# Norm factors of the retention moved from GpSimd to ScalarE and VectorE, and its decay factors made ahead, in a two-layer encoder trunk

## The chip, the cores and the metric

The kernel runs on one core of a Trainium2 chip. The engines are TensorE (PE, matmuls), ScalarE (ACT), VectorE (DVE), GpSimd (POOL) and SyncE (SP, which only issues DMAs). The metric is the device time of one execution, in microseconds, and the change is judged by the median of several executions.

## The reference

Two requests of 512 tokens by 1024 features go through two layers, each x + Mixer(RMSNorm(x)), and a last RMSNorm. The first mixer is differential attention, the second a retention that looks in both directions; both have 8 heads of width 256 in their values, and a gate. The change touches the second only:

```python
def rms_norm(x, g, eps):
    xf = x.astype(jnp.float32)
    y = xf * lax.rsqrt(jnp.mean(xf * xf, axis=-1, keepdims=True) + eps)
    return (y * g.astype(jnp.float32)).astype(x.dtype)
...
def bidir_retention(h, w_in, decay_fwd, decay_bwd, subln_g, w_out):
    B, S, _ = h.shape
    proj = h @ w_in
    q, k, v, gate = jnp.split(proj, [RET_QK_WIDTH, 2 * RET_QK_WIDTH, 2 * RET_QK_WIDTH + D_INNER], axis=-1)
    q = retention_rotate(q.reshape(B, S, N_HEADS, RET_QK_DIM))
    k = retention_rotate(k.reshape(B, S, N_HEADS, RET_QK_DIM)) * (RET_QK_DIM ** -0.5)
    v = v.reshape(B, S, N_HEADS, RET_V_DIM)
    log_g_f = -jnp.exp(decay_fwd.astype(jnp.float32))
    log_g_b = -jnp.exp(decay_bwd.astype(jnp.float32))
    o_f = retention_direction(q, k, v, log_g_f, True)
    o_b = jnp.flip(retention_direction(jnp.flip(q, 1), jnp.flip(k, 1), jnp.flip(v, 1), log_g_b, False), 1)
    o = rms_norm(o_f + o_b, subln_g, SUBLN_EPS)
    o = o.reshape(B, S, D_INNER) * jax.nn.silu(gate)
    return o @ w_out
```

`retention_direction` multiplies the scores of a head with powers of its decay: exp(distance x log_g), with one log_g for keys behind the query and one for keys ahead. The head's output, 256 wide, is normed (divided by the root of its mean square plus 1e-5), gated and projected back. The scale of 256 stands outside the root in the kernel: its factor is (sum of squares + 256 x 1e-5) to the power of -1/2.

## The kernel before, in words

All matmuls are done in three passes: an operand is split into a hi part (a cast on ACT, L437) and a lo part (a subtraction on DVE, L440), and hi x hi, hi x lo and lo x hi are added in a PSUM bank. All large products are done with seven products of half-size blocks instead of eight (P1 to P7, in the order of `SEQ`), whose operands are sums of blocks.

There are four stages: the input and layer 1's projections and attention, until about 1060 us; layer 2's projections; the retention with its output projection, from about 1515 us; and at its end the final norm. The first stage is not touched.

**Projections.** A `Unit` is 256 columns of the weights for both requests. `units2` makes 8 units of q and k, 8 of gates and 4 wide ones of v, and `mixed` interleaves them. `projections` is a generator with one step per product: `prep` makes the operands some steps ahead, `product` the matmuls, `evac` the sums and what follows, and the results go through the ring of slots `os` to DRAM. The last `LEFT` steps (4) are not taken before the retention but in its first rounds, one each. The last unit's bank `z` is taken from the tag "tp".

**Retention.** There are 16 blocks (a head and a request), each with 4 tiles of 128 tokens, so 64 rounds. In a round `score2` makes a tile of scores for the next block (L1228, three matmuls of 512), which DVE multiplies by the decay factors `F` (L1232) and which are split (hi and lo). `av2` multiplies a tile of the present block with v (L1246, twelve matmuls of 256). `norm_stats` has ACT square the result with a sum along the row (L790), and POOL add the constant (L794) and take the power -1/2 (L795). `norm_apply` multiplies the tile by this factor on ACT (L804, into one of two buffers `on`). One round later `turn_o` transposes it on PE (L810) and `gate2` multiplies by the gate on DVE (L1297) and makes the operands of the output projection. `fill` puts one or two output products (`out2`, L1353, six matmuls of 512) into each round.

**Decay factors.** `decay(h)`, called in the retention when a head comes up first, loads the table of distances (448 KB) into `F0` or `F1`, makes on DVE the part of the block on the diagonal (L1209, L1211, L1213) and takes three exponentials on ACT (L1214, L1216, L1218).

**Output weights.** They are split for four heads' worth at a time by `w_split`: P1, P2 and P3 load a block on SP's queue into the tile `wa` or `wb`; P5, P6 and P4 (in `wa`) and P7 (in `wb`) add a block to what stands there, with an accumulating DMA, which POOL issues (L1268, `b<-in_ret_w_out_dram`). Then the sum is split in hi and lo (a cast of 128x1024 on ACT and a subtraction on DVE). Each is made when the old one was used last, so three times in the retention, after the first time at its start. The results of the output products are added to x in DRAM by accumulating DMAs too, issued by POOL at the same line (L1268, `x<-b`) from buffers that DVE (L1378, `put`) or ACT (L1390) writes; for the last heads they are added in SBUF (`evac_last`, L1407), and the final norm follows (L1257).

**What sets the order.** All operations are recorded in a `Plan`, with a cost and what they read and write. `arrange` simulates them and writes down, for each engine, one fixed order: at each step the engine that is free takes the ready operation with the earliest due time. An accumulating DMA costs 1 us of POOL there, lands 5.5 us later, and is held 5 us after it is ready. On the chip each engine works its list in this order: if an operation must wait, all behind it on this engine wait as well.

## Time and profile before

| | us |
|---|---|
| median of the three runs | 1891.86 (1891.03 to 1892.7) |
| profiled execution | 1895.15 |
| its span, first to last instruction | 1893.4 |
| PE busy | 1823.2 (96%) |
| DVE busy | 1462.6 (77%) |
| ACT busy | 967.5 (51%) |
| POOL busy | 230.8 (12%) |
| granted TensorE clock, mean | 0.988 |

An engine that is busy throughout is the limit only in the stretch that the row is for; the views that follow therefore go by stretches of the span. A timeline row gives start, length, engine, line, operation, the tile written and the tiles read; where it has brackets at its end, they hold how long the engine had stood idle and what it waited for. A row of waits gives the engine and line that waited, the engine and line waited for, and then the total in us, the number of times and the longest. A row of groups gives line, engine, operation, tiles and count, then the busy time in us and the mean in ns of one, then the idle time ahead of them. The names `b`, `arena` and `bank` stand for several buffers each.

### The profile page before, as it was taken

How to read it: one execution, taken by the hardware profiler on the slowest of the kernel's cores; microseconds unless marked ns; L12 is line 12 of the kernel's file. 1: busy time of each engine (PE TensorE's matmuls, PEld its weight loads, DVE VectorE, ACT ScalarE, POOL GpSimd, SP SyncE). 2: the span in 40 equal slices, each digit the busy share in tenths (PEclk: the TensorE clock that was granted, in tenths of full speed). 3: DMA queues.
4: the chain of work that ended last, by engine and by line, in shares of the span. 5: the costliest groups of instructions: out<-in, count | busy, mean ns of one | idle time of the engine just before them, and what ended most of it. 6: DMA issues, size and time to landing. Idle time of an engine off the chain costs nothing.

```text
span 1893.4 us, 27928 instructions
## 1 busy us (share of the span) xinstructions
PE 1823.2 (96%) x10241; PEld 1574.5 (83%) x10241; DVE 1462.6 (77%) x2451; ACT 967.5 (51%) x1973; POOL 230.8 (12%) x436
## 2 busy tenths in 40 slices
PE   6999999999999999999999999999999989897977
PEld 5888988988989888888888888989898978786866
DVE  6979688688688688888888887685868677666667
ACT  6744444343343465555556863444444466465543
POOL 2000000000000021111112100000000024443332
PEclk9999999999999999999999999999999999998989
DMA  4345545545445674444452434544455588888884
GB/s 157 119 126 178 167 134 177 157 121 180 156 136 188 250 269 165 178 165 170 178 189 91 138 101 144 167 150 162 145 167 152 194 291 221 217 221 208 237 190 133
DMA packets 161025, 326.18 MB, mean 172 GB/s; under 512 B 13028, under 2 KB 73080, under 8 KB 160888
## 3 DMA queue, kind: packets, MB, share of 16 engines
q1 hardware_dynamic: 149440, 303.36, 48.0%
q0 software_dynamic: 11264, 20.98, 6.9%
q8 instruction: 80, 1.31, 0.3%
q14 instruction: 57, 0.47, 0.1%
q10 hardware_dynamic: 184, 0.08, 0.0%
HBM read 202.72 MB, written 121.63 MB: 171 GB/s over the span
## 4 chain that ended last, share of the span: by engine, by line
PE 83%; DVE 6%; issue 3%; DMA 3%; ACT 3%; POOL 2%; SPq 0%; POOLq 0%; DVEq 0%; ACTq 0%
PE bank L628 36%; PE bank L635 16%; PE bank L879 8%; PE bank L1353 5%; PE bank L1114 5%; PE bank L1062 4%; PE bank L1246 3%; PE bank L1228 2%; PE bank L1098 1%; PE bank L810 1%; DMA b<-in_dist_dram 1%; DVE arena L440 1%; DVE b L440 1%; DMA b<-in_ret_w_out_dram 1%; DVE ws L440 1%
## 5 line engine op out<-in xcount | busy, mean ns | idle before, releaser
L628 PE MATMUL bank<-arena,ws 128*128 128x512 f32 x2160 | 516.1, 393 | 4.9 <-DVE e L495 3.0
L628 PEld LDWEIGHTS bank<-arena,ws 128*128 128x128 f32 x2160 | 405.3, 188 | 93.5 <-ACT ws L437 3.0
L628 PE MATMUL bank<-b,ws 128*128 128x512 f32 x1200 | 293.7, 391 | 0.6 <-DVE e L665 0.6
L628 PEld LDWEIGHTS bank<-b,ws 128*128 128x128 f32 x1200 | 224.7, 188 | 49.7 <-issue 1.0
L794 POOL TENSOR_SCALAR css<-css 128x1 f32<-128x1 f32 x128 | 46.0, 359 | 1522.7 <-ACT bank L792 924.1
L440 DVE TENSOR_TENSOR ws<-st,ws 128x512 fp32r<-128x512 f32 (+1 forms) x192 | 147.9, 775 | 93.3 <-ACT ws L437 59.6
L657 ACT COPY c<-bank 128x512 f32<-128x512 f32 x168 | 98.1, 585 | 219.8 <-PE bank L628 137.3
L635 PE MATMUL bank<-ws,arena 128*128 128x256 f32 x1728 | 207.7, 279 | 0.0
L635 PEld LDWEIGHTS bank<-ws,arena 128*128 128x128 f32 x1728 | 204.6, 188 | 1.3
L879 PE MATMUL bank<-ws,arena 128*128 128x512 f32 x768 | 202.1, 400 | 0.0
L440 DVE TENSOR_TENSOR ws<-raw,ws 128x512 fp32r<-128x512 f32 (+1 forms) x156 | 127.4, 822 | 74.8 <-ACT ws L437 65.7
L437 ACT CAST ws<-st 128x512 fp32r<-128x512 f32 (+1 forms) x192 | 131.9, 693 | 101.2 <-PE bank L628 56.6
L879 PEld LDWEIGHTS bank<-ws,arena 128*128 128x128 f32 x768 | 139.5, 188 | 27.2
L437 ACT CAST ws<-raw 128x512 fp32r<-128x512 f32 (+1 forms) x156 | 114.1, 738 | 75.4 <-PE bank L628 59.3
L665 DVE TENSOR_TENSOR e<-bank,c 128x512 f32<-128x512 f32 x168 | 115.2, 686 | 31.4 <-PE bank L628 24.0
L635 PE MATMUL bank<-ws,b 128*128 128x256 f32 x960 | 118.9, 279 | 0.0
L635 PEld LDWEIGHTS bank<-ws,b 128*128 128x128 f32 x960 | 115.1, 188 | 0.7
L1078 ACT ACTIVATE b<-bank,nm 128x512 f32<-128x512 f32 x128 | 88.1, 688 | 50.5 <-DVE nm L1070 50.4
L884 DVE TENSOR_TENSOR b<-bank,b 128x512 f32<-128x512 f32 x128 | 87.7, 685 | 30.8 <-PE bank L879 30.5
L1114 PE MATMUL bank<-arena 128*128 128x256 f32 x768 | 106.6, 289 | 0.0
L1062 PE MATMUL bank<-arena 128*128 128x512 f32 x384 | 99.9, 396 | 3.4 <-ACT b L1078 3.4
L1070 DVE TENSOR_REDUCE nm<-bank 128x1 f32<-128x512 f32 x128 | 86.6, 687 | 12.6 <-PE bank L1062 12.2
(156 smaller groups left out, 2830.2 us busy)
## 6 DMA issues: line engine op xcount, KB each, us to landing
qk<-os SPq DMA_DIRECT2D x192, 256.0 KB, 3.9
arena<-qk SPq DMA_DIRECT2D x80, 512.0 KB, 5.4
raw<-in_da_w_in_dram SPq DMA_DIRECT2D x64, 512.0 KB, 4.9
v<-os SPq DMA_DIRECT2D x64, 512.0 KB, 3.8
arena<-v SPq DMA_DIRECT2D x48, 512.0 KB, 4.2
raw<-in_ret_w_in_dram SPq DMA_DIRECT2D x48, 512.0 KB, 4.4
g<-e SPq DMA_DIRECT2D x48, 256.0 KB, 4.5
x<-b POOLq DMA_DIRECT2D x48, 256.0 KB, 5.8
```

What stands on the lines that cost most here:

```text
L437: act(n, lambda: nc.scalar.copy(dst(), src()), r, w)
L440: dve(n, lambda: nc.vector.tensor_tensor(dst(), src(), hi().bitcast(F32), op=ALU.subtract), r, w)
L628: nc.tensor.matmul(ps.t, a[u][0]()[:, k, :], bt[k][:, v, :], start=(opens and k == 0 and i == 0), stop=(k == 3 and i == 2), skip_group_che ...
L635: nc.tensor.matmul(ps[:, (t % 2) * 256:(t % 2) * 256 + 256], bt[k][:, v, t * P:(t + 1) * P], a[u][0]()[:, k, :], start=(opens and t % 2 == ...
L657: act(S, lambda c=c, ps=ps: nc.scalar.copy(c.t, ps.t), [ps], [c])
L665: dve(S, lambda e=e, ps=ps, c=c: nc.vector.tensor_tensor(e.t, ps.t, c.t, op=ALU.add), [ps, c], [e])
L879: nc.tensor.matmul(ps.t, o[a][:, e, t * P:(t + 1) * P], u[b][:, e, :], start=(n == 0), stop=(n == 5))
L884: dve(S, lambda: nc.vector.tensor_tensor(half, ps.t, half, op=ALU.add), [ps, (x, i)], [(x, i)])
L1062: nc.tensor.matmul(s.t, q[:, a, t * P:(t + 1) * P], k[:, b, :], start=(n == 0), stop=(n == 2))
L1078: act(840, lambda j=j, s=s, m=m: nc.scalar.activation(p[:, j, :], s.t, AF.Exp, bias=m.t, accum_out=sm[:, j:j + 1]), [s, m], [(p, j), (sm, j)])
L1114: nc.tensor.matmul(o[:, 0:256], aT[:, a, j * P:(j + 1) * P], v[b][:, j, :], start=(n == 0), stop=(n == 11))
L1353: nc.tensor.matmul(ps.t, pick(A[i], u), (hi, lo)[v][:, i, :], start=(opens and n == 0), stop=(n == 5), skip_group_check=True)
```

## The change

1. **Norm.** In the retention, `norm_two` takes the place of `norm_stats`: ACT's Square (L788 of the kernel after), then Sqrt on ACT with the constant as its bias (L790), then on DVE a reciprocal (L791) and three operations of 128x1 for one Newton step (L792, L794, L796). POOL does no norm any more outside layer 1 and the row norms.
2. **Decay factors.** `decay_table(h)` makes the factors of each head in a slot of the `os` ring during the second projections, evenly spread, and stores them in DRAM (`f_d`). `decay(h)` in the retention only loads them.
3. **Units.** `LEFT` is 2. The last wide unit goes to the end of the units; half of its results are put into arena slots 9, 10, 11 and 14 instead of the `os` ring; the bank `z` is that of the others.
4. **Places.** `F0` takes arena slot 3 and the last `aT1` the place `os2`, the other way round than before. A constant `guard` is new.

```diff
...
-LEFT = 4
+LEFT = 2
...
-    LATE = dict(q0=["raw0"], k0=["raw1"], v0=["raw2", "raw3"], aT0=["st0", "st1", "st2", "os0"], sg0=["os1"], F0=["os2"],
-                aT1=[0, 1, 2, 3], k1=[4], q1=[5], v1=[6, 7], AB=[8, 9, 10], sg1=[12], F1=[13], wa=[20], wb=[21], S4=[22],
+    LATE = dict(q0=["raw0"], k0=["raw1"], v0=["raw2", "raw3"], aT0=["st0", "st1", "st2", "os0"], sg0=["os1"], F0=[3],
+                aT1=[0, 1, 2, "os2"], k1=[4], q1=[5], v1=[6, 7], AB=[8, 9, 10], sg1=[12], F1=[13], wa=[20], wb=[21], S4=[22],
...
+    guard = const([P, 1], "guard")
+    dve(4, lambda: nc.vector.memset(guard.t, 256 * SUB_EPS), [], [guard])
...
-            self.z = "sc"
...
-                self.banks[which] = [bank(dict(x="pj", z=self.z, y="o")[which], which) for _ in range(n_banks)]
+                self.banks[which] = [bank(dict(x="pj", z="sc", y="o")[which], which) for _ in range(n_banks)]
...
-    def v_done(dst):
+    def v_done(dst, free=None):
         def done(i, g, tiles, s, psum):
             for u, x in enumerate(tiles):
-                o = os_t()
+                o = slot(next(free), [P, 2, S]) if free and i else os_t()
...
+    def norm_two(o):
+        ss, l, r, t = col(tag="css"), col(tag="crs"), col(tag="crr"), col(tag="cnt")
+        def square():
+            nc.scalar.activation(o[:, 256:512], o[:, 0:256], AF.Square, accum_out=ss.t)
+        act(550, square, [(o, 0)], [(o, 1), ss])
+        plan.op("ACT", 0.22, lambda: nc.scalar.activation(l.t, ss.t, AF.Sqrt, bias=guard.t), [ss, guard], [l])
+        dve(8, lambda: nc.vector.reciprocal(r.t, l.t), [l], [r])
+        dve(8, lambda: nc.vector.scalar_tensor_tensor(
+            t.t, ss.t, 256 * SUB_EPS, r.t, op0=ALU.add, op1=ALU.mult), [ss, r], [t])
+        dve(8, lambda: nc.vector.scalar_tensor_tensor(
+            t.t, t.t, -0.5, r.t, op0=ALU.mult, op1=ALU.mult), [t, r], [t])
+        dve(8, lambda: nc.vector.scalar_tensor_tensor(
+            r.t, t.t, 1.5, r.t, op0=ALU.add, op1=ALU.mult), [t, r], [r])
+        return r
     def norm_stats(o, scale_col=None):
...
+    f_d = [dram([P, 896], f"f{h}") for h in range(NH)]
...
-                      v_done({(i, g): v_d[1, h + i, g] for i in range(2) for g in range(NG)}))
+                      v_done({(i, g): v_d[1, h + i, g] for i in range(2) for g in range(NG)},
+                             iter((9, 10, 11, 14)) if h == NH - 2 else None))
                  for h in range(0, NH, 2)]
-        return mixed(ropes, gates, wides, 2)
+        units = mixed(ropes, gates, wides, 2)
+        last = units.index(wides[-1])
+        units[last:] = units[last + 1:] + units[last:last + 1]
+        return units
...
+    def decay_table(h):
+        t = os_t(F32, "F")
+        Fd = t.t.rearrange("p a s -> p (a s)")
+        dma(lambda: Fd[:, 0:896], lambda: dist_in, [], [t], 448)
+        mid = work("og", [P, P], 2, name="mid")
+        mid2 = work("og", [P, P], 2, name="mid")
+        dve(P, lambda: nc.vector.tensor_scalar(
+            mid.t, Fd[:, 384:512], 0.0, lr[:, 0, h:h + 1], op0=ALU.max, op1=ALU.mult), [t, lr], [mid])
+        dve(P, lambda: nc.vector.tensor_scalar(
+            mid2.t, Fd[:, 384:512], 0.0, lr[:, 1, h:h + 1], op0=ALU.min, op1=ALU.mult), [t, lr], [mid2])
+        dve(P, lambda: nc.vector.tensor_tensor(mid.t, mid.t, mid2.t, op=ALU.add), [mid, mid2], [mid])
+        act(384, lambda: nc.scalar.activation(Fd[:, 0:384], Fd[:, 0:384], AF.Exp, scale=lr[:, 1, h:h + 1]),
+            [lr], [t])
+        act(384, lambda: nc.scalar.activation(Fd[:, 512:896], Fd[:, 512:896], AF.Exp, scale=lr[:, 0, h:h + 1]),
+            [lr], [t])
+        act(P, lambda: nc.scalar.activation(Fd[:, 384:512], mid.t, AF.Exp), [mid], [t])
+        dma(lambda: f_d[h][:], lambda: Fd[:, 0:896], [t], [f_d[h]], 448)
     tab2 = load_tab(rot_tab)
     second_units = units2(tab2)
     step(made, 4)
-    second_units[-1].z = "tp"
     proj = projections(second_units, 12)
     step(proj, 6)
     run(made)
-    step(proj, 7 * len(second_units) - 6 - LEFT)
+    rest = 7 * len(second_units) - 6 - LEFT
+    for h in range(NH):
+        step(proj, rest // NH)
+        decay_table(h)
+    step(proj, rest % NH)
...
     def decay(h):
-        Fd = late(f"F{h % 2}", 0, [P, 896])
-        dma(lambda: Fd.t, lambda: dist_in, [], [Fd], 448)
-        mid = work("og", [P, P], 2, name="mid")
-        mid2 = work("og", [P, P], 2, name="mid")
-        dve(P, lambda: nc.vector.tensor_scalar(
-            mid.t, Fd[:, 384:512], 0.0, lr[:, 0, h:h + 1], op0=ALU.max, op1=ALU.mult), [(Fd, 1), lr], [mid])
-        dve(P, lambda: nc.vector.tensor_scalar(
-            mid2.t, Fd[:, 384:512], 0.0, lr[:, 1, h:h + 1], op0=ALU.min, op1=ALU.mult), [(Fd, 1), lr], [mid2])
-        dve(P, lambda: nc.vector.tensor_tensor(mid.t, mid.t, mid2.t, op=ALU.add), [mid, mid2], [mid])
-        act(384, lambda: nc.scalar.activation(Fd[:, 0:384], Fd[:, 0:384], AF.Exp, scale=lr[:, 1, h:h + 1]),
-            [lr, (Fd, 0)], [(Fd, 0)])
-        act(384, lambda: nc.scalar.activation(Fd[:, 512:896], Fd[:, 512:896], AF.Exp, scale=lr[:, 0, h:h + 1]),
-            [lr, (Fd, 2)], [(Fd, 2)])
-        act(P, lambda: nc.scalar.activation(Fd[:, 384:512], mid.t, AF.Exp), [mid], [(Fd, 1)])
-        Fs[h] = Fd
+        t = Fs[h] = late(f"F{h % 2}", 0, [P, 896], F32R)
+        dma(lambda: t.t.bitcast(F32), lambda: f_d[h][:], [f_d[h]], [t], 448)
     def score2(b, j):
...
-        dve(S, lambda: nc.vector.tensor_tensor(t1.t, s.t, F[:, 384 - P * j:896 - P * j], op=ALU.mult), [s, F], [t1])
+        dve(S, lambda: nc.vector.tensor_tensor(t1.t, s.t, F[:, 384 - P * j:896 - P * j].bitcast(F32), op=ALU.mult), [s, F], [t1])
...
-        ons[b, t] = norm_apply(o, norm_stats(o))
+        ons[b, t] = norm_apply(o, norm_two(o))
     def final_norm(g, t):
```

The orders below show, on three engines, the same place in the program: around the additions of the output weights P7 (tile `b_319` before, `b_321` after) and P6 (`b_304`, `b_306`) for the third set of heads, which is at about 1725 to 1750 us in the trace of before. First POOL before. `css` and `crs` are the sum of squares and the norm factor, `x11` and `x13` are tiles of x in DRAM.

```order
L1268 DMA x11_193<-b_322_14861 128x512
L1268 DMA b_319_14815<-in_ret_w_out_dram 128x2x512
L794 TENSOR_SCALAR css_0_5375<-css_0_5375 128x1
L795 TENSOR_TENSOR crs_0_5388<-css_0_5375,mhalf_0_208 128x1
L1268 DMA b_304_14595<-in_ret_w_out_dram 128x2x512
L1268 DMA x13_195<-b_327_14900 128x512
L1268 DMA x13_195<-b_332_14940 128x512
L794 TENSOR_SCALAR css_1_5427<-css_1_5427 128x1
L795 TENSOR_TENSOR crs_1_5439<-css_1_5427,mhalf_0_208 128x1
```

And POOL after:

```order
L1298 DMA x11_201<-b_324_15024 128x512
L1298 DMA b_321_14971<-in_ret_w_out_dram 128x2x512
L1298 DMA x13_203<-b_329_15061 128x512
L1298 DMA b_306_14737<-in_ret_w_out_dram 128x2x512
L1298 DMA x13_203<-b_334_15104 128x512
L1298 DMA x00_196<-b_341_15172 128x512
L1298 DMA b_306_14737<-in_ret_w_out_dram 128x2x512
L1298 DMA x00_196<-b_346_15283 128x512
```

The norm's two operations have gone from between and behind the additions; the addition to x13 from `b_329` (`b_327` before) now stands ahead of P6's.

ACT at the same place, before. The casts of 128x1024 are the hi parts of P7 and P6, `on` is the normed tile:

```order
L790 ACTIVATE bank_6_296,css_1_5427<-bank_6_296 128x256
L437 CAST b_336_15001<-b_333_14952 128x512
L437 CAST arena_75<-b_340_15012 128x256
L804 ACTIVATE on_1_5212<-bank_6_296,crs_1_5439 128x256
L437 CAST b_325_15027<-b_319_14815 128x1024
L1373 ACTIVATE c_1_423<-bank_2_393 128x512
L437 CAST arena_75<-b_341_15020 128x512
L437 CAST arena_75<-b_304_14595 128x1024
L790 ACTIVATE bank_5_282,css_2_5476<-bank_5_282 128x256
```

And ACT after, where `crr` is the norm factor and `crs` the root:

```order
L788 ACTIVATE bank_6_308,css_1_5437<-bank_6_308 128x256
L790 ACTIVATE crs_1_5449<-css_1_5437,guard_0_223 128x1
L437 CAST b_338_15170<-b_335_15123 128x512
L437 CAST arena_75<-b_342_15177 128x256
L821 ACTIVATE on_1_5222<-bank_6_308,crr_1_5458 128x256
L437 CAST b_327_15195<-b_321_14971 128x1024
L1403 ACTIVATE c_1_434<-bank_2_404 128x512
L437 CAST arena_75<-b_343_15192 128x512
L437 CAST arena_75<-b_306_14737 128x1024
L788 ACTIVATE bank_5_295,css_2_5486<-bank_5_295 128x256
L790 ACTIVATE crs_2_5497<-css_2_5486,guard_0_223 128x1
```

A Sqrt has come behind each Square; the apply, the cast of P7 and the cast of P6 stand in the same order as before, with the next Square behind P6's cast.

DVE at the same place, before. L1209 is a decay factor's operation, the L440 of 128x1024 is the lo part of P7, and L1232 the scores' multiply:

```order
L1378 TENSOR_TENSOR b_339_15005<-c_0_416,bank_1_367 128x512
L1297 TENSOR_TENSOR b_340_15012<-bank_5_282,b_312_14793 128x2x128
L1232 TENSOR_TENSOR b_341_15020<-bank_3_289,b_282_14345 128x512
L440 TENSOR_TENSOR b_336_15001<-b_333_14952,b_336_15001 128x512
L440 TENSOR_TENSOR arena_75<-b_340_15012,arena_75 128x256
L1209 TENSOR_SCALAR og_0_5437<-b_350_14986,lr_0_12798 128x128
L440 TENSOR_TENSOR b_326_15044<-b_319_14815,b_325_15027 128x1024
L440 TENSOR_TENSOR arena_75<-b_341_15020,arena_75 128x512
L1297 TENSOR_TENSOR b_340_15012<-bank_6_296,b_312_14793 128x2x128
```

And DVE after:

```order
L1408 TENSOR_TENSOR b_341_15172<-c_0_427,bank_1_378 128x512
L1327 TENSOR_TENSOR b_342_15177<-bank_5_295,b_314_14948 128x2x128
L791 RECIPROCAL crr_1_5458<-crs_1_5449 128x1
L792 SCALAR_TENSOR_TENSOR cnt_1_13166<-css_1_5437,crr_1_5458 128x1
L794 SCALAR_TENSOR_TENSOR cnt_1_13166<-cnt_1_13166,crr_1_5458 128x1
L796 SCALAR_TENSOR_TENSOR crr_1_5458<-cnt_1_13166,crr_1_5458 128x1
L1262 TENSOR_TENSOR b_343_15192<-bank_4_314,b_283_14495 128x512
L440 TENSOR_TENSOR b_338_15170<-b_335_15123,b_338_15170 128x512
L440 TENSOR_TENSOR arena_75<-b_342_15177,arena_75 128x256
L440 TENSOR_TENSOR b_328_15212<-b_321_14971,b_327_15195 128x1024
L440 TENSOR_TENSOR arena_75<-b_343_15192,arena_75 128x512
L1327 TENSOR_TENSOR b_342_15177<-bank_6_308,b_314_14948 128x2x128
```

The four operations of the norm factor stand between a gate's multiply (L1327) and the scores' multiply (L1262), and the decay factor's operation has gone.

On ACT there is one more load of a function table in the program after than before, right behind the first Square of the retention.

## The prediction

> **What bounds the kernel now.** All times here are of one profiled execution: 1895.15 us, of which 1893.4 us is the span. The median of the runs is 1891.86, so what I work out against the profiled time lies 3.3 us too high for the median, and I take that off at the end.
>
> I read the profile by stage first. The table of windows gives, for each stretch, its length and then the busy time of PE, of its weight loads, of DVE, ACT and POOL (with counts), the granted clock, the DMA share and GB/s.
>
> ```profile
> 1300.00:1515.00 215.00, 215.00 (x1348) 192.87 (x1347) 157.82 (x232) 94.41 (x153) 0.00 (x0) 1.00 0.53 167
> 1528.00:1558.00 30.00, 25.81 (x150) 21.88 (x150) 26.87 (x49) 21.72 (x51) 10.97 (x16) 0.94 0.77 247
> 1558.00:1648.00 90.00, 86.66 (x499) 74.61 (x500) 66.82 (x127) 54.46 (x129) 37.16 (x54) 1.00 0.88 235
> 1657.00:1735.00 78.00, 78.00 (x435) 67.57 (x434) 58.49 (x109) 48.19 (x112) 31.77 (x47) 0.97 0.91 235
> 1835.00:1894.00 59.00, 47.94 (x227) 38.47 (x226) 42.12 (x71) 24.15 (x64) 15.54 (x29) 0.90 0.43 137
> ```
>
> The second projections are bound by PE: it is busy for all 215 us of the second row. So is most of the retention. Between those rows lie three holes, and the waits of the retention (1515 to 1894 us), first those of PE, then of ACT, name them:
>
> ```profile
> PE bank L810 <- ACT on L804: 28.6, 5, 10.1
> ACT on L804 <- POOL crs L795: 54.8, 29, 11.8
> ```
>
> On PE's timeline they look like this (start, length, operation, and in brackets the idle time before it):
>
> ```profile
> 1656.53 0.69 PE L810 MATMUL bank<-ident,on 128*128 128x128 f32 x2 [7.86 <-ACT on L804]
> ...
> 1731.87 0.38 PE L810 MATMUL bank<-ident,on 128*128 128x128 f32 x2
> ...
> 1734.18 1.60 PE L1246 MATMUL bank<-b,b 128*128 128x256 f32 x12
> 1745.84 0.69 PE L810 MATMUL bank<-ident,on 128*128 128x128 f32 x2 [10.06 <-ACT on L804]
> ...
> 1750.17 2.05 PE L1246 MATMUL bank<-b,b 128*128 128x256 f32 x12
> 1752.05 0.40 PE L1353 MATMUL bank<-arena,b 128*128 128x512 f32 x1
> ...
> 1834.82 0.69 PE L810 MATMUL bank<-ident,on 128*128 128x128 f32 x2 [9.18 <-ACT on L804]
> ```
>
> The three stalls are 7.86 + 10.06 + 9.18 = 27.1 us. Each costs more than its length. One round (transposes, scores, six output matmuls, AV) took 1735.78 - 1731.87 = 3.9 us ahead of the stall, and 1752.22 - 1745.84 = 6.4 us behind it: 2.5 us more. So a stall costs about 10 + 2.5 us, and all three about 34.6.
>
> Why does POOL make ACT wait? The POOL timeline around the second stall shows it:
>
> ```profile
> 1725.03 0.93 POOL L1268 DMA_DIRECT2D x<-b  x1
> 1725.77 1.47 POOL L1268 DMA_DIRECT2D b<-in_ret_w_out_dram  x1
> ...
> 1737.08 1.26 POOL L1268 DMA_DIRECT2D b<-in_ret_w_out_dram  x1 [8.51 <-issue]
> ...
> 1743.45 0.88 POOL L1268 DMA_DIRECT2D x<-b  x1 [4.16 <-issue]
> ...
> 1744.71 0.57 POOL L795 TENSOR_TENSOR crs<-css,mhalf 128x1 f32<-128x1 f32 x1
> ```
>
> The norm factor (L795) stands on POOL behind two accumulating loads of output weights (P7's at 1725.77, P6's at 1737.08) and accumulates of x, and these wait in their own issue ("issue", 8.51 and 4.16 us): a second load is not let out until the first is nearly through. The norm does not need those loads; it only queues behind them.
>
> **The norm leaves POOL.** With Sqrt on ACT and the rest on DVE, that wait is gone, all 27.1 us of it as it now stands. What is late next? In ACT's order, before and after, P6's split (hi part, a 128x1024 cast) stands right behind P7's and ahead of the next Square:
>
> ```profile
> 1745.31 0.47 ACT L804 ACTIVATE on<-bank,crs 128x256 f32<-128x256 f32 x1 [11.78 <-POOL crs L795]
> 1745.68 1.04 ACT L437 CAST b<-b 128x1024 fp32r<-128x1024 f32 x1
> ...
> 1747.11 1.56 ACT L437 CAST arena<-b 128x512 fp32r<-128x512 f32 x2
> ```
>
> Then DVE makes the lo part (1.2 us; a 128x1024 piece takes that in the row of DVE two fences below), and PE's output matmuls of P6 follow, which began at 1752.05. So after the change ACT will wait for P6's load itself, and PE for what follows. When does it land? Now P7's load is let out behind an accumulate of x, and that behind a norm; its input, though, was put at 1722.23 + 0.68 = 1722.9:
>
> ```profile
> 1722.23 0.68 DVE L1378 TENSOR_TENSOR b<-c,bank 128x512 f32<-128x512 f32 x1
> 1722.83 1.22 DVE L440 TENSOR_TENSOR arena<-b,arena 128x1024 fp32r<-128x1024 f32 x1
> ```
>
> Without the norm ahead, x goes at 1722.9 and P7's load at 1723.6, 2.2 us earlier. P6's load followed P7's by 11.3 us here, and by 10.5 us at the third stall:
>
> ```profile
> 1815.68 1.59 POOL L1268 DMA_DIRECT2D b<-in_ret_w_out_dram  x1
> ...
> 1826.17 1.26 POOL L1268 DMA_DIRECT2D b<-in_ret_w_out_dram  x1 [7.92 <-DVE b L1407]
> ```
>
> That gives 1734.1 to 1734.9. How long does it take to land? The accumulate behind it got out 6.4 us after it (1743.45 - 1737.08), with PE and most transfers standing still; P4's load, in full traffic, was used 10.0 us after its issue:
>
> ```profile
> 1753.78 1.26 POOL L1268 DMA_DIRECT2D b<-in_ret_w_out_dram  x1
> ```
> ```profile
> 1763.77 1.05 ACT L437 CAST b<-b 128x1024 fp32r<-128x1024 f32 x1 [0.91 <-DMA b<-in_ret_w_out_dram]
> ```
>
> So P6 lands between 1740.5 and 1744.9, and with 1.0 us of hi and 1.2 of lo PE can have it at 1742.7 to 1747.1. PE, not stalled at 1735.78, would be there after one round, at 1739.7. It waits 3.0 to 7.4 us, and begins 5.0 to 9.4 us before 1752.05. Behind the waiting cast stand, on ACT, the Square, the Sqrt and the apply of the next tile, with some 2 us of work down to its transposes on PE; those come one set of output matmuls later, so they are ready at about the time that PE reaches them. A pause slows the matmuls behind it: 2.5 us after ten, and after one of 2.06 us twelve matmuls took 2.54 instead of 1.60:
>
> ```profile
> 1539.05 2.54 PE L1246 MATMUL bank<-b,b 128*128 128x256 f32 x12 [2.06 <-DVE b L1297]
> ```
>
> I take 1 us for that (0.9 to 2.5), the middle of the landing times, and so 7.2 - 1 = 6.2 us a stall: **-18.6** (between 3 x 2.5 = -7.5 and 3 x 8.5 = -25.5).
>
> The Trainium skill ("TensorE: Matmul & The Clock Gate", Part 1) says that the clock falls to half only after an idle window of some 3.4 us. The row of 2.06 us shows a loss without that, so I go by the row; by the rule a rest of 3.0 us would cost nothing, and the sum would be some 3 us lower.
>
> **What the norm costs where it goes.** DVE gets four instructions of 128x1 for each of 64 tiles. The nearest chain is in layer 1:
>
> ```profile
> 710.39 0.17 DVE L1085 RECIPROCAL rc<-sm 128x2 f32<-128x2 f32 x1 [0.49 <-ACT b L1078]
> 710.60 0.27 DVE L1086 TENSOR_SCALAR cc<-sm,rc,neglam 128x1 f32<-128x1 f32 x1
> 710.90 0.75 DVE L1088 SCALAR_TENSOR_TENSOR b<-b,cc 128x512 f32<-128x512 f32 x1
> ```
>
> From start to start that is 0.21 and 0.30 us. Four such are 0.7 (4 x 0.17) to 1.1 us (0.21 + 3 x 0.30); I take 0.9, so 58 us. The decay factors leave this stage:
>
> ```profile
> L1213 DVE TENSOR_TENSOR og<-og,og 128x128 f32<-128x128 f32 x8 | 2.3, 290 | 0.2
> L1214 ACT ACTIVATE b<-b,lr 128x384 f32<-128x384 f32 x8 | 4.9, 610 | 5.7 <-DMA b<-in_dist_dram 5.7
> L1034 ACT ACTIVATE ls<-ls 128x2 f32<-128x2 f32 x1 | 0.2, 205 | 2.5 <-DVE ls L1033 2.5
> L989 ACT ACT_TABLE_LOAD x1 | 1.3, 1283 | 2.5 <-issue 2.5
> ```
>
> Three DVE operations of at most 0.29 for eight heads give 7 us back; DVE gains 51 us of work in a stage where it is off the path. Is there room? A tile passes every 5.5 us: (1894 - 1515 - 27) / 64. The 90 us from 1558 hold 16 to 17 tiles: 66.8 + 16.5 x 0.9 = 82 of 90. There it fits, with little slack, since PE waits whenever the chain is done ahead of a score's multiply, as the order has it. The 30 us from 1528 do not: 26.87 + 5.5 x 0.9 = 31.8, less two heads' factors 1.7, is 30.1 of 30, where PE has 4 us idle already. I put +4 there and +4 on the rest: **+8** (0 if all hides, +51 if none does). The cover is DVE's idle time between PE's results; a tile's chain is no longer than POOL's was (0.44 + 0.66 us on average):
>
> ```profile
> L795 POOL TENSOR_TENSOR crs<-css,mhalf 128x1 f32<-128x1 f32 x64 | 42.2, 659 | 5.4
> ...
> L794 POOL TENSOR_SCALAR css<-css 128x1 f32<-128x1 f32 x64 | 28.1, 439 | 598.4 <-ACT bank L790 598.0
> ```
>
> ACT gets 64 Sqrt of about 0.2 us = 13 us and one more table load of 1.28, and loses 8 x (two of 0.61 and one of about 0.3) = 12: **+0.5**, as it has idle time (54 of 90 busy). The Trainium skill ("ScalarE: Activation LUTs", Table sets) warns that exp and sqrt are in different sets and that each switch costs about 2.7 us with its drain. That rule speaks against a Sqrt among the decay factors' exponentials; here all exponentials come ahead, and the order after has one more load, so by the rule it is 2.7 instead of 1.3, once.
>
> **The decay tables in the projections.** Eight times load, three DVE (0.87), three ACT (1.5) and store: 7 and 12 us on engines that have 57 and 121 us idle in the row from 1300 to 1515. Beside that, what waits behind them: SP's queue carries 16 more transfers, and the output slots are shared with q, k and v's stores. PE is at 100% there, so a late buffer counts in full: **+0.5** (0 to 3). In return the start of the retention finds its table made, and even if that comes no earlier than the distances did, the six operations between it and the first multiply are gone. PE's first scores waited for the multiplies held up by them:
>
> ```profile
> 1525.42 1.69 PE L1228 MATMUL bank<-b,b 128*128 128x512 f32 x6 [0.50 <-DVE b L1232]
> 1528.00 1.67 PE L1228 MATMUL bank<-arena 128*128 128x512 f32 x6 [0.89 <-DVE b L1232]
> ```
>
> **-1.4**. The last units' order, two steps left over instead of four, and the slots that change place: PE does the same matmuls; **+0.5** (0 to 2), two evacuations fewer being spread over the retention's start.
>
> Sum: -18.6 - 1.4 + 8 + 0.5 + 0.5 + 0.5 = -10.5. Against 1895.15 that is 1884.6, and for the median 1881.4, so **1881**, 1875 to 1888 for this case.
>
> **The rivals.**
> First, the stalls go altogether (P6's load is not late at all, since ACT and PE have other work or it is issued much earlier). -34.6 - 1.4 + 9.5 = -26.5: 1865. For it: POOL holds nothing but transfers after the change. Against: 11.3 us between two loads is not the norm's doing. Chance 0.17.
> Second, the wait only changes its name: P6 lands at the late end, 2.5 us are saved each time, and DVE eats them: -7.5 - 1.4 + 9.5 = +0.6, so 1892, spread 1888 to 1897. This is also the case that the change does not do what it says. For it: 88% to 91% DMA share in those stages. Chance 0.20.
> Third, slower: DVE becomes the retention's limit. The chain stands in order ahead of a score's multiply, for which PE waits; if the 0.9 us comes in series for every tile, +51 instead of +8, and -18.6 - 1.4 + 51 + 1.5 = +32: 1924. It decides from the point where DVE is over nine tenths busy in the windows from 1558 and 1657. Against: 82 of 90. Chance 0.12, with smaller forms of it between 1896 and 1910.
>
> **Numbers.** Forecast 0.51, rivals 0.17, 0.20, 0.12. The measurement tells apart 0.2%, 3.8 us: same is 1888.1 to 1895.6. Faster: 0.17, 0.46 of the forecast and a little of the second, 0.64; same 0.18; slower 0.18. The range, 1863 to 1898, holds all but the third rival and the ends.
>
> **What would show it.** Right: no ACT wait for POOL at the apply; three waits of 3 to 7 us at PE's output matmuls, with ACT's cast waiting for the weights' DMA; DVE at 88% to 92% from 1558. The Newton chain near 0.9 us; one more table load. Wrong: PE waiting for DVE by over 15 us more in all, or P6's issue not 2 us earlier against PE's work, or the projections over 2 us longer.

## The result

The changed kernel takes 1869.64 us (median of four, 1861.33 to 1877.63) where the kernel before took 1891.44 (four, 1889.42 to 1892.7): a ratio of 0.9885, with an interval of 0.9839 to 0.9932. Two later sets of six executions, each beside the kernel before on the same chip, gave 0.9895 (0.9871 to 0.9918) and 0.9902 (0.9881 to 0.9923). So the change saves 18 to 22 us. The forecast was 1881 us, the range 1863 to 1898: the time lies in the range, but below the 1875 to 1888 given for the forecast itself, and the gain is about twice the one forecast.

The profiled execution of the changed kernel is its fastest, 1861.33 us with a span of 1859.6. That is 33.8 us less than the profiled one of before, and not all of it is the change's. To see where it comes from, I take four places in both traces: the first matmul of the second projections, the first score, the start of each of the 64 AV groups of PE (the twelve matmuls of `av2`), and the end of the last matmul. PE does the same amount of work between them, with one exception: ahead of the 10th AV group it makes 16 tiles of scores before and 14 after. The two others, six matmuls or about 1.6 us (three take 0.78 us from start to start), come in the next stretch.

| stretch, us | before | after | difference |
|---|---|---|---|
| start to second projections | 1061.5 | 1052.5 | -9.0 |
| second projections to first score | 453.6 | 453.7 | +0.1 |
| first score to 10th AV group | 50.5 | 45.4 | -5.1 |
| three stalls: 27th to 29th, 43rd to 45th, 59th to 61st AV group | 21.0 + 23.0 + 21.3 | 14.9 + 14.1 + 13.6 | -22.7 |
| the three stretches ahead of these | 81.4 + 66.1 + 66.9 | 82.7 + 67.4 + 66.1 | +1.9 |
| 61st AV group to last matmul | 40.2 | 41.8 | +1.6 |
| last matmul to the end | 7.9 | 7.3 | -0.6 |

The first row is layer 1, which the change does not touch. The experiments below show that its length differs from one execution to the next. The retention, from the first score to the last matmul, fell from 370.4 to 346.1 us.

The windows, cut around the same stretches (length, busy time of PE, weight loads, DVE, ACT and POOL with counts, granted clock, DMA share, GB/s), first that of the first stall before, then those of the changed kernel:

```profile
1648.00:1657.00 9.00, 1.14 (x9) 0.94 (x7) 0.00 (x0) 1.00 (x2) 3.94 (x5) 0.73 0.72 107
```

```profile
1536.00:1634.00 98.00, 94.58 (x550) 80.77 (x549) 86.31 (x226) 66.94 (x164) 19.42 (x21) 1.00 0.92 243
1634.00:1644.00 10.00, 7.10 (x42) 5.72 (x41) 5.96 (x14) 4.80 (x11) 2.92 (x3) 1.00 1.02 257
...
1717.00:1726.00 9.00, 6.88 (x40) 5.41 (x39) 5.81 (x13) 4.71 (x11) 2.54 (x3) 1.00 0.96 216
...
1797.00:1807.00 10.00, 7.98 (x41) 6.89 (x41) 7.11 (x15) 6.74 (x15) 2.14 (x2) 0.83 0.90 210
```

Most of each hole has closed: in the 10 us around the first stall PE now works 7.1 us, where it worked 1.1 of 9 before. DVE, the second busiest engine before as well, is now busy for 86 of 98 us, where it was for 67 of 90. Who PE waits for now, in the retention, the three longest rows (engine and line, what it waited for, total, times, longest), and who the apply on ACT waits for:

```profile
PE bank L1276 <- DVE b L1327: 5.6, 7, 1.5
PE bank L1383 <- ACT arena L437: 3.5, 2, 2.1
PE bank L827 <- ACT on L821: 3.4, 4, 2.0
```
```profile
ACT on L821 <- DVE crr L796: 34.8, 47, 2.1
```

The apply does not wait for POOL any more. The second row of PE is the wait that the prediction put in its place, at two of the three stalls: output matmuls wait for P6's cast. ACT's timeline at the second place, and PE's:

```profile
1717.13 1.05 ACT L437 CAST b<-b 128x1024 fp32r<-128x1024 f32 x1
...
1722.38 1.04 ACT L437 CAST arena<-b 128x1024 fp32r<-128x1024 f32 x1 [3.20 <-DMA b<-in_ret_w_out_dram]
1723.33 0.37 ACT L788 ACTIVATE bank<-bank 128x256 f32<-128x256 f32 x1
```
```profile
1720.43 1.69 PE L1276 MATMUL bank<-b,b 128*128 128x256 f32 x12
1723.48 0.50 PE L1383 MATMUL bank<-arena,b 128*128 128x512 f32 x1 [1.36 <-ACT arena L437]
1724.74 0.50 PE L1383 MATMUL bank<-b,b 128*128 128x512 f32 x1 [0.76 <-DVE b L440]
...
1727.84 1.66 PE L1383 MATMUL bank<-b,b 128*128 128x512 f32 x6 [0.76 <-ACT c L1403]
```

ACT stands 3.2 us for the DMA itself, with the next Square behind it, and PE 1.4 and 0.8 us for the hi and the lo part. POOL's timeline shows when the loads went out:

```profile
1705.37 1.23 POOL L1298 DMA_DIRECT2D b<-in_ret_w_out_dram  x1 [2.78 <-DVE b L440]
...
1716.54 1.21 POOL L1298 DMA_DIRECT2D b<-in_ret_w_out_dram  x1 [5.20 <-DVE cnt L794]
```

P7's and then P6's: 11.2 us apart, nearly as before (11.3), and P6 landed 1722.38 - 1716.54 = 5.8 us after its issue. The bracket of P6's row names the engine whose event came last by the profile, not what held the load: by the trace's landing times P7's load had landed 0.3 us before. The norm's operations, as groups of DVE and ACT (mean ns behind the total):

```profile
L791 DVE RECIPROCAL crr<-crs 128x1 f32<-128x1 f32 x64 | 10.1, 157 | 11.7 <-ACT crs L790 11.6
L792 DVE SCALAR_TENSOR_TENSOR cnt<-css,crr 128x1 f32<-128x1 f32 x64 | 10.2, 159 | 2.2
```
```profile
L790 ACT ACTIVATE crs<-css,guard 128x1 f32<-128x1 f32 x64 | 18.8, 294 | 1.9
L790 ACT ACT_TABLE_LOAD x1 | 1.3, 1283 | 0.0
```

### The profile page after: what moved, and what is told of

The parts are those of the page before. It is cut to its first block, busy times and chain, and to the rows that moved or that the text cites. A ratio compares the mean times of both kernels' runs of the same rounds, so it can differ in the third digit from the quotient of the medians.

```text
span 1859.6 us, 28097 instructions
## 1 busy us (share of the span) xinstructions
PE 1809.8 (97%) x10241; PEld 1561.3 (84%) x10241; DVE 1495.3 (80%) x2708; ACT 987.3 (53%) x2038; POOL 159.5 (9%) x308
## 4 chain that ended last, share of the span: by engine, by line
PE 80%; DVE 6%; issue 6%; DMA 3%; ACT 3%; POOL 2%; SPq 0%; POOLq 0%; DVEq 0%; ACTq 0%
PE bank L629 39%; PE bank L636 16%; PE bank L896 9%; PE bank L1136 5%; PE bank L1084 4%; PE bank L1383 3%; DMA b<-in_ret_w_out_dram 2%; PE bank L1120 1%; PE bank L1276 1%; DVE b L440 1%; PE bank L827 1%; DVE arena L440 1%; POOL x L1298 1%; PE bank L1258 1%; ACT arena L437 1%
## 5 line engine op out<-in xcount | busy, mean ns | idle before, releaser
L440 DVE TENSOR_TENSOR ws<-st,ws 128x512 fp32r<-128x512 f32 (+1 forms) x192 | 147.9, 774 | 85.3 <-ACT ws L437 56.7
L440 DVE TENSOR_TENSOR ws<-raw,ws 128x512 fp32r<-128x512 f32 (+1 forms) x156 | 127.4, 822 | 75.5 <-ACT ws L437 60.5
L437 ACT CAST ws<-raw 128x512 fp32r<-128x512 f32 (+1 forms) x156 | 114.1, 737 | 72.7 <-PE bank L629 52.9
L811 POOL TENSOR_SCALAR css<-css 128x1 f32<-128x1 f32 x64 | 18.5, 289 | 917.2 <-ACT bank L809 916.9
```

The source lines that it names most:

```text
L437: act(n, lambda: nc.scalar.copy(dst(), src()), r, w)
L440: dve(n, lambda: nc.vector.tensor_tensor(dst(), src(), hi().bitcast(F32), op=ALU.subtract), r, w)
```

## The experiments

My theory is that the gain comes from the norm leaving POOL's queue of accumulating loads, that the tables made ahead matter because they spare table loads on ACT, and that what is left is P6's load. The rivals are that the tables themselves bring the gain, that DVE is about to become the limit, and, for the 9 us of layer 1, that the program's layout has changed. The retention's length below is from the first score to the last matmul of the profiled execution.

| kernel | ratio to before (interval) | retention, us | second projections begin at |
|---|---|---|---|
| before | | 370.4 | 1061.5 |
| after | 0.9885 (0.9839 to 0.9932) | 346.1 | 1052.5 |
| e1, after again | 0.9895 (0.9871 to 0.9918) | 346.5 | 1056.1 |
| e2, guard only | 0.9993 (0.9978 to 1.0008) | 368.4 | 1053.4 |
| e3, norm only | 1.0003 (0.9988 to 1.0018) | 373.3 | 1056.1 |
| e4, tables only | 0.9996 (0.9977 to 1.0015) | 368.9 | 1055.1 |
| e5, norm only, one table | 0.9856 (0.984 to 0.9871) | 345.0 | 1056.7 |
| e6, two Newton steps | 0.9924 (0.9907 to 0.9941) | 358.4 | 1056.7 |
| e7, later landing in the plan | 0.9962 (0.9942 to 0.9982) | 361.4 | 1055.4 |
| e8, before, plain loads | 0.9794 (0.9777 to 0.9811) | 331.0 | 1058.9 |
| e9, no Newton step | 0.9862 (0.9837 to 0.9886) | 339.1 | 1060.4 |
| e10, P6 first | 0.9893 (0.987 to 0.9916) | 349.0 | 1062.2 |
| e11, after, third time | 0.9902 (0.9881 to 0.9923) | 353.7 | 1054.0 |
| e12, P6 first, no Newton step | 0.9883 (0.9858 to 0.9909) | 344.1 | 1060.8 |

e1 to e4 ran on one chip, e5 to e8 on a second, e9 to e12 on a third, each set beside the kernel before.

**e1.** No edit: the changed kernel again.

> The changed kernel once more, as it is. In the profile of the changed kernel the retention gained 24.8 us and layer 1, which the change does not touch, 9.0 us (its wide products of 96 matmuls took 0.4 us less). If those 9 us are a trait of the program (another layout of its constants, by the new one), this profile shows layer 1 ending at 1052 us again. If they are a trait of the execution, it ends anywhere from 1052 to 1062 us, and the times spread as the four did, 1861 to 1878 us, with the retention itself the same to 2 us. Median expected: 1870 us.

Median 1871.16 us (1865.39 to 1877.59). Layer 1 ended at 1056.1 us this time, between the two; the retention was 346.5. So the 9 us are a trait of the execution.

**e2.** The constant alone, in the kernel before:

```diff
+    guard = const([P, 1], "guard")
+    dve(4, lambda: nc.vector.memset(guard.t, 256 * SUB_EPS), [], [guard])
```

> The kernel before with nothing but the new constant (one column, unused). Layout theory: layer 1 is 9 us shorter, 1882 us, with a spread like that of the changed kernel. Theory that the execution decides: as before, 1891 us, layer 1 ending at 1061 to 1062 us.

No difference in time. Its profiled execution had layer 1 end at 1053.4 us, which by itself would have spoken for the layout; its median is that of before, 1889.31 against 1890.42. So the layout theory falls: over the fourteen profiles of all kernels here that point lies anywhere from 1052 to 1062 us, and the constant alone changes no median.

**e3.** The norm change alone:

```diff
-        ons[b, t] = norm_apply(o, norm_stats(o))
+        ons[b, t] = norm_apply(o, norm_two(o))
```

> The norm change alone; the decay factors are still made in the retention, so exponentials and square roots alternate on ACT and the program has 24 table loads instead of 2. Queue theory (the stalls come from the norm standing behind the weights' accumulating loads on POOL): the three stalls shrink as in the changed kernel, -22 us; the 22 more loads take 22 x 1.28 = 28 us of ACT's idle time, of which a third may reach PE: 1878 us, from 1870 (all hidden) to 1895 (all on the path). Rival (the gain comes from the tables made ahead): no gain from the norm, and the loads on top: 1900 us or more.

Ratio 1.0003: between the two, nearer to "all loads on the path". PE's wait for the apply falls from 28.6 to 6.9 us, yet the first two stalls' places are still 21.0 and 20.4 us long: what is gained is paid back. The groups of ACT with the table loads (two of the six groups), and one of them on ACT's timeline:

```profile
L791 ACT ACT_TABLE_LOAD x12 | 15.4, 1283 | 0.2
...
L1232 ACT ACT_TABLE_LOAD x6 | 7.7, 1283 | 0.1
```
```profile
1593.76 0.18 ACT L789 ACTIVATION_READ_ACCUMULATOR bank<-bank 128x1 f32 x1
1593.96 1.28 ACT L791 ACT_TABLE_LOAD   x1
1595.26 0.29 ACT L791 ACTIVATE crs<-css,guard 128x1 f32<-128x1 f32 x1
1596.37 0.47 ACT L822 ACTIVATE on<-bank,crr 128x256 f32<-128x256 f32 x1 [0.81 <-DVE crr L797]
```

A load of 1.28 us stands between the sum of squares and its root, thus in the norm's chain. Of the 23 additional ones, twelve are in such a place, ten ahead of a decay factor and one ahead of a gate's tanh (L735).

**e4.** Everything but the norm:

```diff
-        ons[b, t] = norm_apply(o, norm_two(o))
+        ons[b, t] = norm_apply(o, norm_stats(o))
```

> Everything but the norm: tables made in the projections, units and slots as in the changed kernel, but the norm on POOL. Queue theory: the three stalls of 8 to 10 us stay as they were, only the start of the retention gains 1 to 4 us: 1888 us (1885 to 1892). Rival (the tables bring the gain): 1870 us.

Ratio 0.9996, and the wait of the kernel before is there in full:

```profile
PE bank L827 <- ACT on L821: 30.5, 5, 10.3
```

The tables, the units' order and the places bring nothing that these executions can tell. The rival that they bring the gain falls.

**e5.** e3 without the table loads. The norm factor is left out by it: the operations are all there, their value is not.

```diff
-        plan.op("ACT", 0.22, lambda: nc.scalar.activation(l.t, ss.t, AF.Sqrt, bias=guard.t), [ss, guard], [l])
+        plan.op("ACT", 0.22, lambda: nc.scalar.activation(l.t, ss.t, AF.Identity, bias=guard.t), [ss, guard], [l])
```

> The norm change alone, with the decay factors still made in the retention, but with an identity in place of the square root, so that ACT keeps one table (1 load in the program instead of 24). The norm factor is left out by this: every operation of it is there, its value is not. If the norm change alone gained nothing because of the 23 more table loads, this kernel gains what the changed one does in the retention, less the start: ratio 0.989 to 0.992, retention (first score to the last matmul) 347 to 351 us instead of 373. If it gained nothing because the decay factors' own work stands in the way of the norm, the retention stays at 365 us or more and the ratio at 0.997 to 1.001.

Ratio 0.9856, retention 345.0: 28.3 us less than e3, for 23 table loads that are gone (23 x 1.283 = 29.5); the order on every engine is the same in both. So on average the loads cost nearly their length, and the tables made ahead are worth about that: nothing alone (e4), 28 us beside a Sqrt. The Trainium skill gives the reason ("ScalarE: Activation LUTs", Table sets: exp and sqrt lie in different sets, work should be batched by set). Its price of about 2.7 us for a switch, load and drain together, is not seen here: 28.3 / 23 = 1.23 us each, and the root began 1.30 us after the start of its load, before which ACT stood idle for 0.02 us.

The cost is not even, though: the first two stalls' places hold six of the loads and lose 12.1 us, with a lower granted clock there as well (0.67 and 0.75, in e5 0.89 and 1.00), while the third holds none and loses nothing.

**e6.** A second Newton step:

```diff
+        dve(8, lambda: nc.vector.scalar_tensor_tensor(
+            t.t, ss.t, 256 * SUB_EPS, r.t, op0=ALU.add, op1=ALU.mult), [ss, r], [t])
+        dve(8, lambda: nc.vector.scalar_tensor_tensor(
+            t.t, t.t, -0.5, r.t, op0=ALU.mult, op1=ALU.mult), [t, r], [t])
+        dve(8, lambda: nc.vector.scalar_tensor_tensor(
+            r.t, t.t, 1.5, r.t, op0=ALU.add, op1=ALU.mult), [t, r], [r])
```

> The changed kernel with a second Newton step, three more DVE operations of 0.16 us in each of 64 tiles: 0.19 x 3 x 64 = 37 us more work on DVE, and 0.58 us more in each tile's chain. If DVE's idle time covers the norm, as the first comparison suggests (the stretches between the stalls grew by under 2 us for 50 us of new work), this costs 0 to 5 us: ratio to before 0.990 to 0.993. If DVE is near its limit, the next 37 us are paid for by half or more: ratio 1.00 or above.

Ratio 0.9924, inside the first expectation and 4 to 5 us above the two later sets of the changed kernel, with intervals that overlap; its retention is 358.4, longer by 12 us than in the two fastest profiles and by 5 than in e11. So some 5 to 12 of 37 us are paid. PE's waits in the retention are 26.1 us in all instead of 20.1, and the longest row is that of the AV groups that wait for the gate's multiply (5.6 in 7 waits without the second step):

```profile
PE bank L1282 <- DVE b L1333: 7.7, 16, 1.1
```

DVE is not the limit, and its idle time is no full cover either. The operations added also made the planner put others in another order, here and in e9, so that not all of either difference need be DVE's work.

**e7.** One number of the planner:

```diff
-            dma_add(lambda: t.t, lambda: w_block(p, e, i), [t], [t], 512)
+            dma_add(lambda: t.t, lambda: w_block(p, e, i), [t], [t], 512, hold=5.0, lands=10.0)
```

> The changed kernel with one number of the planner changed: it takes the weights' accumulating loads to land 10 us after their issue instead of 5.5, so P6's cast stands behind the next Square and apply on ACT, and its matmuls later on PE. If what is left of the stalls is P6's landing (2 to 3 us of waits on PE at each, and what follows), it goes: 9 to 12 us less than the changed kernel, ratio to before 0.983 to 0.985. If the waits only move to another product, ratio 0.988 to 0.990 as now.

A miss on both sides: 0.9962, 11 to 15 us slower than the changed kernel. The stalls' places became short (7.6, 7.6 and 8.9 us), but the stretches behind them grew by more (29th to 43rd AV group 73.7 us instead of 67.4, 45th to 59th 78.3 instead of 66.1, 61st to the last matmul 52.9 instead of 41.8): the additions came later, and other waits grew:

```profile
PE bank L1276 <- DVE b L1327: 7.4, 10, 2.3
PE bank L1383 <- ACT b L437: 3.9, 1, 3.9
PE bank L1383 <- DVE b L440: 3.2, 6, 0.9
```

Which of them decides I did not find out.

**e8.** The kernel before, with the four additions as plain loads on SP's queue. The sums of blocks are left out by it.

```diff
-            dma_add(lambda: t.t, lambda: w_block(p, e, i), [t], [t], 512)
+            dma(lambda: t.t, lambda: w_block(p, e, i), [], [t], 512)
```

> The kernel before, norm on POOL, but P5, P6, P7 and P4's weights are loaded on SP's queue in place of being accumulated by POOL. The sums of blocks are left out by this, so the outputs are not the reference's. If the norm only waits because the accumulating loads stand ahead of it on POOL, the three stalls go (no more than 3 us of PE waits at the transposes): 25 to 33 us less, ratio 0.983 to 0.987. If POOL's norm is itself too slow, or the accumulates of x hold it as well, the stalls shrink by half at most: ratio 0.992 or above.

Ratio 0.9794, beyond the 25 to 33 us that I expected (38.0), with the norm still on POOL. The wait at the transposes went from 28.6 to 2.8 us:

```profile
PE bank L810 <- ACT on L804: 2.8, 4, 1.0
```

So POOL is fast enough for the norm, its accumulates of x do not hold it, and without the accumulating loads of weights there are no stalls. As plain loads the weights also come earlier, so e8 alone does not tell the norm's place in the queue from the weights' lateness; e5 does, where the loads are accumulating as before and PE's wait at the transposes is 3.9 us. The retention of 331 us is also the least that any kernel here reached, against 346 to 354 of the changed kernel; the difference is not the loads' alone, as the changed kernel has the norm's work on DVE too.

**e9.** The changed kernel without its three Newton operations (the refinement is left out):

```diff
-        dve(8, lambda: nc.vector.scalar_tensor_tensor(
-            t.t, ss.t, 256 * SUB_EPS, r.t, op0=ALU.add, op1=ALU.mult), [ss, r], [t])
-        dve(8, lambda: nc.vector.scalar_tensor_tensor(
-            t.t, t.t, -0.5, r.t, op0=ALU.mult, op1=ALU.mult), [t, r], [t])
-        dve(8, lambda: nc.vector.scalar_tensor_tensor(
-            r.t, t.t, 1.5, r.t, op0=ALU.add, op1=ALU.mult), [t, r], [r])
```

> The changed kernel without the Newton step: the norm factor is the reciprocal of ACT's root alone, so three DVE operations a tile less (64 x 3 x 0.19 = 37 us). The refinement is left out. A second step cost 12 us for the same 37 us of work. If DVE's load is what is paid for, and more for each step, the first step costs less than the second: 2 to 6 us faster than the changed kernel. If DVE's load before that is fully covered: 0 to 1 us.

1863.42 against 1871.86 us of the changed kernel on the same chip (e11): 8.4 us, more than the 2 to 6 expected. The retention is 7 us shorter than in the changed kernel's fastest profile, and PE's waits for the gate's multiply fell from 5.6 to 2.3 us:

```profile
PE bank L1270 <- DVE b L1321: 2.3, 5, 0.6
```

It is faster than the kernel before and the changed one; of the other kernels only two have a lower ratio, and these leave out the norm factor (e5) or the sums of blocks (e8).

**e10.** P6's addition ahead of P7's on POOL, by a dependency that only the planner sees:

```diff
-            dma_add(lambda: t.t, lambda: w_block(p, e, i), [t], [t], 512)
+            first = op == "P7"
+            dma_add(lambda: t.t, lambda: w_block(p, e, i), [t, wa["wa"]] if first else [t], [t], 512, 0.0 if first else 5.0)
```

> The changed kernel with P6's accumulating load ahead of P7's on POOL. In the traces P6's load was issued 0.2 to 0.3 us after P7's had landed, 10 us later than its tile was free, while PE needs P6 first. If what is left of the stalls is this queue, the waits of PE at P6's matmuls (2.9 to 3.7 us at each place) and the matmuls slowed behind them go: 8 to 12 us less than the changed kernel. If P7 and P4, now later by as much, take P6's place as the late ones: no gain, 0 +- 3 us.

1869.95 against 1871.86: the second expectation. The places of the stalls became 5 to 6 us shorter (27th to 29th AV group 8.9 instead of 14.9 us), and the stretch behind the first grew by 8.8 (29th to 37th: 47.0 instead of 38.2). POOL, ACT and PE there:

```profile
1645.42 1.21 POOL L1298 DMA_DIRECT2D b<-in_ret_w_out_dram  x1 [1.69 <-issue]
1658.65 1.21 POOL L1298 DMA_DIRECT2D b<-in_ret_w_out_dram  x1 [1.75 <-ACT c L1404]
```
```profile
1655.75 1.04 ACT L437 CAST b<-b 128x1024 fp32r<-128x1024 f32 x1 [6.50 <-DMA b<-in_ret_w_out_dram]
```
```profile
1656.85 0.50 PE L1384 MATMUL bank<-b,b 128*128 128x512 f32 x1 [4.40 <-ACT b L437]
```

Now P7's load, issued at 1645.42, is the late one: its cast waits 6.5 us, PE 4.4. So it is the sequence of additions, one behind the other, that is late, whichever of them stands first.

**e11.** No edit: the changed kernel beside e9, e10 and e12.

> The changed kernel as it is, beside the others on the same chip: 1861 to 1878 us, ratio to before 0.988 to 0.990. Its retention (first score to the last matmul) 346 to 347 us in the profile.

The time is as expected, the retention is not: 353.7 us, 7 more than in the other two profiles. The difference begins at the first set of weights, ahead of the first stall. First this kernel's PE, then its ACT, then ACT in the first profile:

```profile
1531.76 2.20 PE L1276 MATMUL bank<-b,b 128*128 128x256 f32 x12 [2.80 <-DVE b L1327]
...
1573.86 1.01 PE L1276 MATMUL bank<-arena 128*128 128x256 f32 x3 [3.78 <-DVE b L1327]
```
```profile
1571.17 1.04 ACT L437 CAST b<-b 128x1024 fp32r<-128x1024 f32 x1 [3.83 <-DMA b<-in_ret_w_out_dram]
```
```profile
1563.56 1.05 ACT L437 CAST b<-b 128x1024 fp32r<-128x1024 f32 x1 [0.29 <-DMA b<-in_ret_w_out_dram]
```

An accumulating load came 3.5 us later for ACT than in the first profile, and PE waited 3.8 us and then ran three matmuls in 1.01 instead of 0.62 us. That accounts for part of the 7 us only: all of PE's waits in the retention are 22.8 us here and 20.1 in the first profile, and PE's busy time for the same matmuls is 330.7 us instead of 325.9, at a granted clock of 0.98 instead of 1.00. So the executions of the changed kernel differ in the retention too, by when these loads land and by whether a wait lowers the clock; the fast profile shows the change at its best, and the medians lie above it.

**e12.** e9 and e10 together.

> P6's load ahead of P7's and no Newton step (the refinement is left out). If the two costs are separate, the gains add: 10 to 18 us less than the changed kernel. If the waits for DVE and for P6 cover each other, no more than the larger of the two.

Ratio 0.9883, 2.8 us less than e11 and more than e9 alone: the gains do not add. The intervals of e9 and e12 overlap, so it is not shown that e12 is the slower one.

## Why the prediction came out as it did

**What bounds.** The reading of the stalls held. The norm stood in POOL's queue behind the weights' additions: without the additions (e8) or with the norm elsewhere (e5) the waits for it go, with everything else changed and the norm on POOL (e4) they stay.

**What is late next.** Held at two of the three places: ACT's cast waits for P6's DMA, 3.20 us at the second (shown above) and 3.99 at the first. At the third it was another wait, one that the prediction did not have: ACT stands 2.83 us for the gain of the final norm, which comes on SP's queue and which ACT did not have to wait for in the kernel before; the apply behind it is late, and PE's transposes with it. P6's cast follows with 0.38 us. The first place, then the third:

```profile
1640.83 1.04 ACT L437 CAST arena<-b 128x1024 fp32r<-128x1024 f32 x1 [3.99 <-DMA b<-in_ret_w_out_dram]
...
1798.59 0.63 ACT L1464 ACTIVATE cos<-cos 128x512 f32<-128x512 f32 x1 [2.83 <-DMA cos<-in_final_norm_g_dram]
...
1803.17 1.04 ACT L437 CAST arena<-b 128x1024 fp32r<-128x1024 f32 x1 [0.38 <-DMA b<-in_ret_w_out_dram]
```

POOL let the loads out there like this, P5's, P7's, P6's and P4's at the first place, and P7's and P6's at the third:

```profile
1609.60 1.22 POOL L1298 DMA_DIRECT2D b<-in_ret_w_out_dram  x1 [4.03 <-DVE b L1327]
...
1623.03 1.21 POOL L1298 DMA_DIRECT2D b<-in_ret_w_out_dram  x1 [2.21 <-DVE b L440]
1633.92 1.22 POOL L1298 DMA_DIRECT2D b<-in_ret_w_out_dram  x1 [5.62 <-DVE crr L791]
...
1644.60 1.22 POOL L1298 DMA_DIRECT2D b<-in_ret_w_out_dram  x1 [2.61 <-DVE b L1262]
...
1785.61 1.23 POOL L1298 DMA_DIRECT2D b<-in_ret_w_out_dram  x1 [1.45 <-DVE b L440]
1797.11 1.23 POOL L1298 DMA_DIRECT2D b<-in_ret_w_out_dram  x1 [5.09 <-DVE crr L796]
```

P6's load was forecast to go out 10.5 to 11.3 us after P7's and did so 10.9, 11.2 and 11.5 us after it. Against PE's work, the AV group ahead of the stall, it went out 1.3, 3.0 and 1.9 us earlier than before, where 2.2 were forecast. **The size was the error.** I took the middle of 6.4 and 10.0 us for the landing; it was 6.9, 5.8 and 6.1. PE waited 2.1 + 0.8 us at the first place and 1.4 + 0.8 at the second instead of the 5.2 of the sum, and the stalls gave 22.7 us instead of 18.6. The 22.7 is inside the bounds that stood there, 7.5 to 25.5. The lower end came from P6's own load in the kernel before, at the same place, the upper one from P4's, in another stretch; the own one was the nearer. That the third place came out near the others is luck, as its wait was not the one in the sum.

The clock's part came out mixed. In the third place, PE's timeline shows a wait of 2.0 us, with slowed matmuls behind it:

```profile
1800.46 0.44 PE L827 MATMUL bank<-ident,on 128*128 128x128 f32 x2 [2.02 <-ACT on L821]
...
1801.43 2.51 PE L1383 MATMUL bank<-b,b 128*128 128x512 f32 x6
```

and the granted clock of that window is 0.83. Behind the wait of 2.1 us in the first place it is 1.00 throughout. In e11 it is 0.83 over the 10 us around a wait of 1.94 us at the same first place. That the same wait costs clock in one execution and not in another fits a window that runs by itself, as the Trainium skill has it ("TensorE: Matmul & The Clock Gate", Part 1); that it takes some 3.4 us of idling is not what these rows show.

**DVE, +8.** One operation is 0.16 us, and a chain goes at 0.19 a step (0.77 instead of 0.9). Against the kernel before, the stretches between the stalls and the tail grew by 1.9 + 1.6 = 3.5 us, less than half of the term, and 1.6 us of them are the score matmuls that moved. PE's waits for DVE in the retention are 10.6 us in all, as before (10.4). But e9 is 8.4 us faster without the Newton step, in part at the start and in the stalls, where the table of stretches counts such a cost with other gains. So the cost of DVE's work may well have had the size of the term, and what the sum left out is a gain beside it. The stretch from the first score to the 10th AV group shows that gain: 5.1 us less instead of the forecast +4 - 1.4. Of the 5.1, 1.6 are the moved score matmuls, so 3.5 are left, and the same stretch took 49.0 instead of 50.5 in e2, the kernel before but for a constant. With the tables and not the norm it is 47.3 us (e4), with both 45.4. The -1.4 came out: PE's waits for the scores' multiply in the retention fell from 2.3 to 0.7 us. Where the rest comes from was not isolated. In e8, which differs from the kernel before by the loads alone (and also has 14 tiles of scores here), it is 44.1: so the accumulating loads cost something in this stretch too, which the sum did not count.

**ACT, +0.5.** The Sqrt took 0.29 us instead of 0.2, 6 us more in all, on an engine that is busy for 67 of the 98 us from 1536. The additional table load is one. That the tables made ahead are the condition for this came out stronger than the prediction had it: it put the alternation aside because the order after does not have it, and e3 against e5 gives its price, 28 us.

**Projections and units, +0.5 each.** 0.1 us measured from the second projections to the first score. Eight tables more cost nothing there. (PE is busy for all 215 us in the first row of the prediction's windows, not in the second, as its text has it.)

**The rivals.** The first, all stalls gone at 1865 us, is nearer to the median than the forecast, but its reason did not hold: the stalls' places are still 13.6 to 14.9 us long, where e8 without the loads takes 10.3 for the same two AV groups at the first and at the second place. The second and third did not come about; with 37 us more of DVE's work (e6) the retention grew by 5 to 12 us, so the third was still some way off.

So the mechanism held for the stalls, and two terms had the wrong size: the landing time in the stalls' sum, and the start of the retention, put at a loss together with DVE where it was a gain. Both errors point the same way, and it is the width of the range that kept the time inside it.

What stays open: why e5, with the factors made in the retention and one table, has a lower ratio than the changed kernel (0.9856 against 0.9885 to 0.9902, on different chips); where the gain at the start of the retention comes from; and whether a second addition could be let out while the first is on its way, which no run here tried to bring about.

## What to carry to other kernels

An engine's queue that issues slow transfers is a poor place for a short step of a chain, however idle the engine is on average: look at what stands ahead of it in order, not at its 12%. When such a step moves to ACT, ask first which function tables it alternates with; here 23 loads of 1.28 us cost 28 us. And when a wait goes, the next one is found by following the order past it, at each place anew; for its size, take the row of the same transfer at the same place, if there is one, ahead of a row from another stretch.

## What the runs showed of the hardware that I had not expected

Accumulating loads of 512 KB from POOL went one after the other: in the changed kernel P6's was issued at 1716.54, 11.2 us after P7's and 0.3 us after P7's had landed, though nothing else in the order stood between but an accumulate of x. In none of the thirteen traces that have such loads were two of them under way at once, while a load and a 256 KB accumulate of x often were. The four of a set go out over 35.0 us (1609.60 to 1644.60), and plain loads in their place took 38 us off the kernel before (e8, without the sums). Waits of PE of about 2 us lowered the granted clock in some cases and not in others: 2.02 us at the third place to 0.83 over 10 us, 2.14 us at the first not at all (1.00). And layer 1 ended at 1052.5, 1054.0 and 1056.1 us in the three profiles of the changed kernel, and between 1052 and 1062 us in all fourteen, without any change to its work.
